# A Hymba block on one core: the first half's input projection on the input times the norm's weight, its row factors applied behind it, and another order of loads and background work

## The chip, the cores and the metric

One core of a Trainium2 chip runs the whole program. The time is device microseconds of one execution. The kernel before was run three times; its median is 2093.23 us.

## The reference

The kernel computes one decoder block in float32 on 2048 positions of width 1024. Cut to what matters for the change:

```python
h = rmsnorm(x, norm1_g)                    # x * rsqrt(mean(x^2) + 1e-6) * norm1_g
proj = h @ w_in
p_q, p_k, p_v, p_g, p_a, c_b, c_c, c_h = split(proj)

log_a = log_sigmoid(p_a @ w_gate_up + b_gate) / 16          # the gate
o = gla_chunked(q, k, v, log_a)            # chunks of 64, a state carried along
o = rmsnorm(o, gla_norm_g) * silu(p_g)
o_conv = c_b * causal_depthwise_conv(c_c * c_h, conv_w)     # width 3

x = x + concat([o, o_conv]) @ w_out
h2 = rmsnorm(x, norm2_g)
x = x + (silu(h2 @ w_ffn_gate) * (h2 @ w_ffn_up)) @ w_ffn_down
return rmsnorm(x, norm_f_g)
```

The norm's row factor rsqrt(mean(x^2) + 1e-6), one number for each position, can be taken out of the product: proj is that factor times ((x * norm1_g) @ w_in).

## The kernel before

**Arithmetic.** A float32 product is made of three matmuls in a rounded format: each operand is split into a high and a low half (`split`, lines 152 to 154: ACT copies the source into the high half, DVE subtracts that from the source for the low half), and TensorE adds high x high, high x low and low x high. A main matmul has 128x128 weights and 128x512 of the other operand.

**Units.** Positions are worked on in two halves of two blocks of 512. The input projection has twelve units (`unit`, the weights of one unit are 1 MB, four quarters of 128x512 each). Ten units of the first half and all of the second make a 2x2 block product from seven products of sums and differences (84 main matmuls); POOL makes the sums and differences of weights (`unit_weights`), and those of the operands are called T1 to T4. The first two units of the first half are plain, 96 main matmuls each: `build_first` (lines 288 to 328) makes the operands of the half as it goes and multiplies them, and `plain_unit` (line 330) is the second. The differences of the operands (line 325, POOL) are made behind these.

**The start.** `first_loads` (line 486) loads for each of the two blocks four tiles of rows (128x1024) and eight tiles of the transposed input (`h`, 128x512), with the first unit's weights between. ACT squares the rows and adds them up (line 484); `rows_rstd` (line 469) makes the row factor from these sums, spreads it over 128x128 tiles (`rep`, line 477) and transposes them on TensorE into a PSUM bank `rb_ps`. `scaled` (line 510, DVE) multiplies each h tile by the norm's weight and by that factor; the result is split into `op`, the operand of the first unit.

**Background work.** Python generators stand in a list; after each product a `tick` takes steps from the first of them. In the list stand the gate's weights, nine empty steps, `row_stats` of the second half's two blocks (row squares and factors), `gate(0)`, and `h1_ahead`, which makes the second half's operands, B11 to T4, and writes them to memory. `gate` has 32 matmuls into `a_ps` (line 578) and then eight into `z` (line 591); from z, `forget_gate` (lines 597 to 614) makes the decay by ACT and DVE with a scan (line 607) and stores it (`sd`). `gla_half` then runs through the first half's chunks: it loads kq, the decay `ee`, vt and gt (lines 695 to 707), DVE multiplies kq by the decay (lines 703 and 704), TensorE makes the scores `sc` (line 714) and transposes (lines 720 and 723), and so on.

**What sets the order.** The program is traced in Python's order and then scheduled once, at build time, by a simulated timeline; each engine runs its own instructions in that fixed order, and waits on semaphores. SP issues all loads and stores, in order, and blocks on the first that has to wait.

## Time and profile before

| | us |
|---|---|
| median of three executions | 2093.23 |
| the three executions | 2089.54, 2093.23, 2095.66 |
| the profiled execution | 2092.78 |
| its span | 2090.8 |
| start of TensorE's first main matmul | 18.43 |
| end of the second plain unit (192 main matmuls) | 78.5 |
| last main matmul of the first half's input projection (1032) | 288.5 |
| TensorE's granted clock over the span | 0.993 of full |

The span runs from the first to the last instruction of the profile; 2.0 us of the execution's time lie around it. A row of the profile names an engine (PE is TensorE, PEld its weight loads, DVE VectorE, ACT ScalarE, POOL GpSimd, SP SyncE), a line of the kernel, an operation and its tiles, output before input. A row of the timeline begins with its start and its length in us; "x2" behind it is the number of instructions that were put together, and in brackets stands how long the engine was idle before it and what ended that. A row of the waits names the waiting engine and line, the one it waited for, the sum in us, the number of waits and the longest. A row of the busy windows gives the window, its length, then each engine's busy time with its number of instructions, the granted clock, the share of the DMA engines and GB/s. TensorE's matmuls overlap, so the length of one in the timeline is longer than the step from one to the next.

### The profile page before, as it was taken

Reading aid. Unit: us, or ns where it says so; the run is one execution under the profiler, and the core shown is the slowest. Engines: PE = TensorE matmul, PEld = TensorE weight load, DVE = VectorE, ACT = ScalarE, POOL = GpSimd, SP = SyncE. Lnnn points to the kernel's source line nnn. Section 1 sums busy time; section 2 is a strip of 40 time slices with the busy share of each in tenths; the row PEclk is TensorE's granted clock in tenths of the full one; section 3 lists DMA queues with packets and bytes.
Section 4 is the critical chain, followed back from the end, with each engine's and each line's share of the span. In section 5 each row is a group of like instructions: output and inputs, shape, how many; then the busy total and the mean of one; then the engine's idle time right before and its main releaser. Section 6 shows DMA issues by size and latency. Waiting matters only on the chain.

```text
span 2090.8 us, 26872 instructions
## 1 busy us (share of the span) xinstructions
PE 2029.0 (97%) x9133; PEld 1648.4 (79%) x9133; DVE 1434.0 (69%) x2049; ACT 970.1 (46%) x1921; POOL 876.7 (42%) x637
## 2 busy tenths in 40 slices
PE   5999999999999999999999999999999999999996
PEld 4778888887888887778788878887888888878884
DVE  6669786549754696787887566654776767666665
ACT  5555455656543345454555442223455444453234
POOL 3427222122102464555555434533655544434543
PEclk9999999999999999999999999999999999999998
DMA  7349485424586882654654587698454465488672
GB/s 275 126 152 307 154 338 162 146 96 145 181 306 212 329 286 93 230 224 174 227 222 171 214 326 280 235 358 349 146 206 158 169 228 191 164 349 307 267 272 111
DMA packets 189241, 464.43 MB, mean 222 GB/s; under 512 B 19824, under 2 KB 65072, under 8 KB 179504
## 3 DMA queue, kind: packets, MB, share of 16 engines
q1 hardware_dynamic: 189104, 462.72, 61.3%
q8 instruction: 72, 1.18, 0.2%
q14 instruction: 65, 0.53, 0.1%
HBM read 297.49 MB, written 165.15 MB: 221 GB/s over the span
## 4 chain that ended last, share of the span: by engine, by line
PE 77%; DVE 10%; DMA 6%; issue 3%; ACT 2%; POOL 2%; SPq 1%; DVEq 0%; ACTq 0%; POOLq 0%
PE mm L381 22%; PE mm L383 22%; PE mm L382 22%; DVE wq L154 2%; DVE h L510 2%; PE mm L814 2%; PE mm L815 2%; PE mm L817 2%; DMA op<-shT 1%; DVE so L154 1%; DVE op L154 1%; PE a_ps L578 1%; DMA shT<-so 1%; SPq L145 1%; PE o_ps L738 1%
## 5 line engine op out<-in xcount | busy, mean ns | idle before, releaser
L381 PE MATMUL mm<-op,wq 128*128 128x512 f32 x2499 | 979.6, 394 | 11.0 <-ACT wq L153 4.2
L382 PE MATMUL mm<-op,wq 128*128 128x512 f32 x2499 | 974.5, 390 | 0.0
L383 PE MATMUL mm<-op,wq 128*128 128x512 f32 x2499 | 962.4, 391 | 11.7 <-DVE wq L154 11.2
L154 DVE TENSOR_TENSOR wq<-raw,wq 128x512 fp32r<-128x512 f32 (+2 forms) x626 | 506.7, 815 | 243.2 <-ACT wq L153 241.4
L153 ACT ACTIVATE wq<-raw 128x512 fp32r<-128x512 f32 (+2 forms) x626 | 365.0, 588 | 600.5 <-PE mm L383 461.9
L381 PEld LDWEIGHTS mm<-op,wq 128*128 128x128 f32 x2499 | 469.9, 188 | 123.4 <-ACT wq L153 10.3
L383 PEld LDWEIGHTS mm<-op,wq 128*128 128x128 f32 x2499 | 469.8, 188 | 119.8 <-DVE wq L154 21.5
L382 PEld LDWEIGHTS mm<-op,wq 128*128 128x128 f32 x2499 | 470.1, 188 | 96.5 <-issue 1.0
L366 POOL TENSOR_TENSOR raw<-s,raw 128x512 f32<-128x512 f32 (+2 forms) x97 | 126.5, 1304 | 468.2 <-DVE wq L154 446.9
L364 POOL TENSOR_TENSOR s<-raw 128x512 f32<-128x512 f32 (+2 forms) x97 | 127.2, 1311 | 219.5 <-DMA raw<-in_wffn_dram 95.1
L407 DVE TENSOR_TENSOR y<-mm,y 128x512 f32<-128x512 f32 x185 | 127.4, 689 | 123.3 <-PE mm L383 122.6
L371 POOL TENSOR_TENSOR raw<-raw 128x512 f32<-128x512 f32 (+2 forms) x97 | 125.4, 1292 | 166.0 <-DVE wq L154 158.8
L407 DVE TENSOR_TENSOR c<-mm,c 128x512 f32<-128x512 f32 x198 | 135.6, 685 | 64.6 <-PE mm L383 63.3
L796 POOL TENSOR_TENSOR ssx<-ssx,q 128x512 f32<-128x512 f32 x52 | 76.2, 1479 | 160.7 <-ACT q L795 160.5
L365 POOL TENSOR_TENSOR raw<-raw 128x512 f32<-128x512 f32 (+2 forms) x97 | 136.5, 1407 | 4.9
L403 ACT ACTIVATE c<-mm 128x512 f32<-128x512 f32 x198 | 114.8, 586 | 16.2 <-PE mm L383 14.8
L154 DVE TENSOR_TENSOR so<-t,so 128x512 fp32r<-128x512 f32 x100 | 90.9, 914 | 27.3 <-ACT so L153 26.7
L153 ACT ACTIVATE wq<-s 128x512 fp32r<-128x512 f32 (+2 forms) x97 | 56.8, 585 | 96.2 <-PE mm L383 92.7
L814 PE MATMUL mm<-op,wq 128*128 128x512 f32 x256 | 100.9, 395 | 0.0
L815 PE MATMUL mm<-op,wq 128*128 128x512 f32 x256 | 99.8, 390 | 0.0
L154 DVE TENSOR_TENSOR wq<-s,wq 128x512 fp32r<-128x512 f32 (+2 forms) x97 | 79.7, 822 | 4.1 <-ACT wq L153 3.5
L153 ACT ACTIVATE so<-t 128x512 fp32r<-128x512 f32 x100 | 62.4, 626 | 42.1 <-DMA sa_B<-so 17.8
(178 smaller groups left out, 1849.8 us busy)
## 6 DMA issues: line engine op xcount, KB each, us to landing
raw<-in_wffn_dram SPq DMA_DIRECT2D x44, 1024.0 KB, 5.7
sa_T<-so SPq DMA_DIRECT2D x88, 512.0 KB, 4.9
op<-sa_T SPq DMA_DIRECT2D x88, 512.0 KB, 8.9
sa_B<-so SPq DMA_DIRECT2D x69, 512.0 KB, 3.5
op<-sa_B SPq DMA_DIRECT2D x69, 512.0 KB, 9.2
raw<-in_win_dram SPq DMA_DIRECT2D x23, 1024.0 KB, 5.6
raw<-in_wdown_dram SPq DMA_DIRECT2D x24, 768.0 KB, 5.9
sx<-y SPq DMA_DIRECT2D x48, 256.0 KB, 3.2
```

Source lines behind the costliest of these rows:

```text
L153: last_hi[:] = [act.activation(hi, src, AF.Copy)]
L154: return dve.tensor_tensor(lo, src, hi.bitcast(F32), ALU.subtract)
L364: pool.tensor_tensor(s1, a21, a22, ALU.add)
L365: pool.tensor_tensor(a21, a11, a21, ALU.subtract)
L366: pool.tensor_tensor(a11, s1, a11, ALU.subtract)
L371: pool.tensor_tensor(a12, a12, a11, ALU.subtract)
L381: pe.matmul(o[:], wh, xh, start=first and k == 0, stop=False, skip_group_check=True)
L382: pe.matmul(o[:], wh, xl, start=False, stop=False, skip_group_check=True)
L383: return pe.matmul(o[:], wl, xh, start=False, stop=k == n - 1, skip_group_check=True)
L407: dve.tensor_tensor(t[:], o[:], t[:], ALU.add)
L814: pe.matmul(o[e, j][:], wh, m[:, 0, :], start=k == 0, stop=False)
L815: pe.matmul(o[e, j][:], wh, m[:, 1, :], start=False, stop=False)
```

## The change

The first half's projection no longer waits for the row factors: ACT and DVE split x times the norm's weight straight away (lines 317 and 320 of the changed file), and POOL scales the h tiles in place for the later differences (line 323). The row factor `factors` is multiplied in behind the product, only where a result needs it: on units 4, 5, 6 and 9 (`factored`, line 560; for 6 and 9 its square), on the gate's `a_sb`, on the convolution's y, on v (its square as ACT's scale) and in the GLA's own norm. q and k stay without it up to there. The loads come in another order (weights and h first, the second unit's weights ahead of the last h tiles, row tiles last), the row squares move into the background (`first_stats`), and 18 matmuls of 128x128 on a tile of ones stand ahead of everything. In the list of the background `gate(0)` is now last, behind all of `h1_ahead`.

```diff
-    def build_first(quad, w):
+    def build_first(h, raw):
 ...
+        def turn(n, i):
+            with ExitStack() as stack:
+                if order:
+                    stack.enter_context(tc.issue_after(order[-1].ins))
+                w[n] = weight_quarter(raw[:, i, :])
+            order.append(last_hi[0])
 ...
             for k in range(KD):
-                with ExitStack() as stack:
-                    if len(los) > 1:
-                        stack.enter_context(tc.issue_after(los[-2].ins))
-                    h[k, j] = quad(k, j)
+                g = col(C_G1 + k)
+                if j == 0 and k in (0, 3, 4):
+                    turn(*{0: ("A11", 0), 3: ("A12", 1), 4: ("A22", 2)}[k])
                 x = opp.tile([P, 2, PB], F32R, name="op", tag="op")
-                los.append(split(h[k, j][:], x[:, 0, :], x[:, 1, :]))
-                if j == 0 and k >= PT:
-                    row_squares(1, k - PT)
+                with tc.issue_after(order[-1].ins):
+                    order.append(act.activation(x[:, 0, :], h[k, j][:], AF.Copy, scale=g))
+                if (k, j) == (0, 0):
+                    turn("A21", 3)
+                dve.scalar_tensor_tensor(
+                    x[:, 1, :], h[k, j][:], g, x[:, 0, :].bitcast(F32), ALU.mult, ALU.subtract
+                )
+                pool.tensor_scalar(h[k, j][:], h[k, j][:], g, 1.0, ALU.mult, ALU.mult)
 ...
-            if j == 0:
-                rbs[1] = rows_rstd(squares[1])
+            out += [(r, j, settled(o[r, j], True), False) for r in range(2)]
 ...
+    def first_stats():
+        yield from pause(1)
+        for b in range(2):
+            for t in range(PT):
+                row_squares(b, t)
+                if t % 2:
+                    yield
+        yield from pause(3)
+        for b in range(2):
+            f, f2 = [mtiny.tile([P, PT], F32, name=n, tag=f"{n}{b}", bufs=1) for n in ("f", "ff")]
+            factors[b] = tiny.tile([P, PB], F32, name="rb", tag="rb")
+            act.activation(factors[b][:], rows_rstd(squares[b], f)[:], AF.Copy)
+            dve.tensor_tensor(f2[:], f[:], f[:], ALU.mult)
+            positions[b] = f, f2
+            yield
 ...
         raw = rawp.tile([P, 4, PB], F32, name="raw", tag="raw")
+        for j in range(2):
+            for k in range(KD):
+                if j == 0 and k % 4 == 0:
+                    for i in ((0, 3), (1, 2))[k // 4]:
+                        raw_loads.append(load(raw[:, i, :], win[0][:, i, :]))
+                if (j, k) == (1, 2):
+                    second = raw_weights(win[1])
+                h = raws[k, j] = bt("h") if len(raws) > 4 else tt("h")
+                load(h[:], xt[j, :, k, :])
 ...
+    def factored(c, in_psum, f):
+
+        s = tt("n") if in_psum else c
+        (dve if in_psum else pool).tensor_tensor(s[:], c[:], f[:], ALU.mult)
+        return s
 ...
         a_sb = bt("a_sb")
-        act.activation(a_sb[:], a[:], AF.Copy)
+        if half:
+            act.activation(a_sb[:], a[:], AF.Copy)
+        else:
+            for j in range(2):
+                r = slice(32 * j, 32 * j + 32)
+                dve.tensor_tensor(a_sb[r, :], a[r, :], factors[j][r, :], ALU.mult)
 ...
+        def values(u):
+            f = factors2 if u in (6, 9) else factors
+            for r, j, c, p in next(units):
+                if half == 0 and u in (4, 5, 6, 9):
+                    c, p = factored(c, p, f[j]), False
+                yield r, j, c, p
 ...
+                    if half == 0:
+                        pool.tensor_tensor(y[:], y[:], factors[j][:], ALU.mult)
 ...
-        act.activation(v[:], v_ps[:], AF.Copy)
+        if b in positions:
+            act.activation(v[:], v_ps[:], AF.Copy, scale=positions[b][1][:, t : t + 1])
+        else:
+            act.activation(v[:], v_ps[:], AF.Copy)
 ...
-            act.activation(sq[:], o[:, h, :], AF.Square, accum_out=ssq[:, h : h + 1])
+            f = positions[b][0][:, t : t + 1] if b in positions else 1.0
+            act.activation(sq[:], o[:, h, :], AF.Square, scale=f, accum_out=ssq[:, h : h + 1])
 ...
+    warm = bank("warm")
+    for _ in range(18):
+        pe.matmul(warm[:, 0:P], ones[:], ones[:], start=True, stop=True)
 ...
     background.extend(
         [
-            gate_weights(), pause(9), row_stats(2), row_stats(3), gate(0, ops), unhurried(),
-            h1_ahead(),
+            gate_weights(), first_stats(), pause(3), row_stats(2), row_stats(3), begun(h1, 10),
+            unhurried(), h1, gate(0, ops),
         ]
     )
```

Where instructions stand, at two places.

**The second unit's weights on ACT, early in the program.** Line 153 makes high halves (`wq` of weights, `op` of operands), line 484 or 515 squares rows, line 432 or 446 copies a result. Before, the last splits of the first unit's operands and the first two weights of the second unit:

```order
L153 ACTIVATE op_697<-h_512 128x512
L153 ACTIVATE op_707<-h_514 128x512
L464 ACTIVATE xn_1037,ssq_1036<-xn_1037 128x512
L153 ACTIVATE op_717<-h_516 128x512
L464 ACTIVATE xn_1038,ssq_1036<-xn_1038 128x512
L432 ACTIVATE c11_807<-mm_567 128x512
L153 ACTIVATE op_727<-h_518 128x512
L153 ACTIVATE wq_818<-raw_816 128x512
L153 ACTIVATE wq_821<-raw_816 128x512
```

And now, from the fourth of the eight row squares to the same two weights:

```order
L515 ACTIVATE xr_534,ssq_527<-xr_534 128x1024
L153 ACTIVATE op_734<-h_491 128x512
L515 ACTIVATE xr_537,ssq_536<-xr_537 128x1024
L153 ACTIVATE op_738<-h_493 128x512
L446 ACTIVATE c11_643<-mm_549 128x512
L515 ACTIVATE xr_539,ssq_536<-xr_539 128x1024
L446 ACTIVATE c11_645<-mm_550 128x512
L515 ACTIVATE xr_541,ssq_536<-xr_541 128x1024
L158 ACTIVATE rl_1000<-f_997 128x4
L153 ACTIVATE op_742<-h_495 128x512
L515 ACTIVATE xr_543,ssq_536<-xr_543 128x1024
L153 ACTIVATE wq_785<-raw_513 128x512
```

The row squares, which stood ahead of the first unit, stand between its last split and the second unit's first weights; op_734 and op_738 are splits of differences that POOL makes behind its scalings.

**The first half's gate and the first GLA chunk.** On TensorE, before, inside the eleventh unit, between its product on op_642 and its next one on op_773:

```order
L383 MATMUL mm<-op,wq 128x512
L714 MATMUL sc<-kq 128x128 x4
L720 MATMUL kt_ps<-ident,kq 128x128 x2
L723 MATMUL v_ps<-ident,vt 128x128 x2
L381 MATMUL mm<-op,wq 128x512
```

Now, ahead of the last product of the twelfth unit (op_922 to op_934, twelve matmuls), the last two z matmuls:

```order
L623 MATMUL z_2719<-a_sb_2591,wgu_sb_101 128x512
L623 MATMUL z_2761<-a_sb_2591,wgu_sb_101 128x512
L395 MATMUL mm_2545<-op_922,wq_2542 128x512
L396 MATMUL mm_2545<-op_922,wq_2542 128x512
L397 MATMUL mm_2545<-op_922,wq_2542 128x512
```

and behind that product the scores, followed by the second half's first matmul (op_2820 is its first operand):

```order
L397 MATMUL mm<-op,wq 128x512
L757 MATMUL sc<-kq 128x128 x4
L763 MATMUL kt_ps<-ident,kq 128x128 x2
L766 MATMUL v_ps<-ident,vt 128x128 x4
L395 MATMUL mm<-op,wq 128x512
```

On DVE, before, the two steps on the kq that these scores read (kq_2726) stand among the last steps of the convolution in the tenth unit (L655) and weight splits:

```order
L655 SCALAR_TENSOR_TENSOR c12_1818<-u_2046,sml_99,c12_1818 128x512 x2
L154 TENSOR_TENSOR wq_2081<-raw_2066,wq_2081 128x512
L703 TENSOR_TENSOR kq_2726<-kq_2726,ee_2727 128x256
L704 SCALAR_TENSOR_TENSOR kq_2726<-kq_2726,ee_2727 128x256
L154 TENSOR_TENSOR wq_2084<-raw_2066,wq_2084 128x512
```

Now the two steps on their kq (kq_2780), with the end of what stands between them and the step that reads z_2719 (thirty rows earlier); g2 is the decay, `op` the second half's operands:

```order
L643 TENSOR_TENSOR g2_2764<-g1_2763 128x512
L154 TENSOR_TENSOR op_2868<-op_2868 128x512
L154 TENSOR_TENSOR op_2872<-op_2872 128x512
L645 TENSOR_TENSOR dn_2717<-em_2716,el_2718 128x4
L154 TENSOR_TENSOR op_2876<-op_2876 128x512
L645 TENSOR_TENSOR dn_2717<-em_2716,el_2718 128x4
L154 TENSOR_TENSOR op_2880<-op_2880 128x512
L154 TENSOR_TENSOR op_2884<-op_2884 128x512
L154 TENSOR_TENSOR op_2888<-op_2888 128x512
L154 TENSOR_TENSOR op_2892<-op_2892 128x512
L154 TENSOR_TENSOR op_2896<-op_2896 128x512
L746 TENSOR_TENSOR kq_2780<-kq_2780,ee_2781 128x256
```

On SP the load of the second part of ee_2781 now stands behind two stores of the decay:

```order
L148 DMA sd1_1_131<-g2_2764 128x512
L145 DMA gt_2783<-sg0_2_154 128x128
L145 DMA gt_2783<-sg0_3_155 128x128
L145 DMA kq_2956<-sk0_0_112 128x128
L145 DMA ee_2781<-sd0_1_129 128x128
```

The gate's 32 a_ps matmuls and eight z matmuls, which stood behind main matmuls 312 to 384, stand now behind 938 to 1020. From main matmul 1056 on, TensorE's order is the same in both programs.

More of the change, by code (lines that the diff above doesn't have):

```diff
@@ L225, in unhurried, with begun @@
         yield
+    def begun(work, n):
+        for _ in range(n):
+            next(work)
+            yield
     def pause(n):
@@ L479, in rows_rstd @@
         return rb_ps
-    rbs, raws, first_weights, last_load, rows, squares = {}, {}, {}, [], {}, {}
+    rbs, raws, positions, rows, squares, factors, factors2 = {}, {}, {}, {}, {}, {}, {}
     def row_squares(b, t):
@@ L495, in first_loads @@
                 load(xr[:], x[r0 : r0 + P, :])
[L496 to L507 removed]
+        return raw, second
     def scaled(g, rb, h):
@@ L614, in forget_gate, with in_proj @@
         store(s_d[b][i][:], t2[:])
-    def in_proj(half, ops, first=None, differences=None):
+    def in_proj(half, ops, first=None, second=None, differences=None):
+        def values(u):
[4 more added lines that the diff above has]
+                yield r, j, c, p
         def units():
             for u in range(12):
-                with ExitStack() as stack:
-                    if half == 0 and u == 1:
-                        stack.enter_context(tc.issue_after(last_load[0].ins))
-                    if half or u > 1:
-                        us = unit(win[u], ops)
-                    else:
-                        us = plain_unit(win[u], ops) if u else first
+                if half or u > 1:
+                    us = unit(win[u], ops)
+                else:
+                    us = plain_unit(second, ops) if u else first
                 if half == 0 and u == 1:
```

58 lines of the change are left out of this document (26 added, 32 removed).

## The prediction

> **What bounds the kernel now.** First the busy times and the share of each engine in the chain that ended last, then the waits of TensorE:
>
> ```profile
> PE 2029.0 (97%) x9133; PEld 1648.4 (79%) x9133; DVE 1434.0 (69%) x2049; ACT 970.1 (46%) x1921; POOL 876.7 (42%) x637
> PE 77%; DVE 10%; DMA 6%; issue 3%; ACT 2%; POOL 2%; SPq 1%; DVEq 0%; ACTq 0%; POOLq 0%
> PE rb_ps L478 <- DVE rep L477: 15.7, 2, 15.5
> PE mm L383 <- DVE wq L154: 11.2, 10, 2.7
> ```
>
> TensorE works for 97% of the span, and two items carry most of its waiting: 15.5 us ahead of the first transposes (the row norm at the start) and 11.2 us in ten waits for low halves of weights. The busy windows of the part that the change reorders, cut where TensorE has issued 0, 96+96 (two plain units), 276, 864, 1032 and 1056 of its main 128x512 matmuls, say where that waiting lies (columns: length, then PE, PEld, DVE, ACT, POOL busy, granted clock, DMA share, GB/s):
>
> ```profile
> 0.00:18.40 18.40, 1.34 (x4) 0.65 (x4) 6.32 (x20) 9.02 (x17) 1.11 (x7) 1.00 0.87 299
> 18.40:78.50 60.10, 52.46 (x196) 40.16 (x197) 54.55 (x74) 39.67 (x94) 31.99 (x21) 0.94 0.64 222
> 78.50:97.80 19.30, 19.30 (x87) 15.93 (x87) 9.23 (x17) 6.36 (x11) 5.17 (x4) 1.00 0.31 110
> 97.80:248.80 151.00, 148.68 (x635) 118.74 (x635) 117.49 (x162) 75.78 (x140) 67.54 (x44) 0.99 0.63 209
> 248.80:288.50 39.70, 39.70 (x184) 32.60 (x183) 25.91 (x38) 16.77 (x35) 9.11 (x6) 1.00 0.61 235
> 288.50:295.50 7.00, 7.00 (x41) 5.78 (x39) 4.57 (x6) 2.79 (x7) 4.00 (x3) 1.00 1.04 401
> ```
>
> From 78.5 us on TensorE is full but for 2.3 us. One unit of 84 matmuls takes 19.3 us with its three transposes, or 0.227 us a matmul. Before that, 192 matmuls (43.6 us at this pitch) need 78.5 us: 34.9 us are lost, 18.4 of them before the first. In the second row DVE is busy for 54.55 of 60.10 us: there DVE, not TensorE, sets the pace.
>
> After main matmul 1056 the order of TensorE is the same in both programs to the last row. So the forecast is the time at which matmul 1056 is reached: 295.5 us now.
>
> **Two prices that the sum needs.** DVE and POOL hold each other up. The same split of 128x512 and the same three-element work of DVE, with POOL idle (first two rows) and with POOL at its differences (the rest):
>
> ```profile
> 27.75 1.29 DVE L154 TENSOR_TENSOR op<-h,op 128x512 fp32r<-128x512 f32 x2
> 27.46 0.16 DVE L472 TENSOR_SCALAR msq<-ssq 128x4 f32<-128x4 f32 x1
> 51.19 6.99 DVE L154 TENSOR_TENSOR op<-h,op 128x512 fp32r<-128x512 f32 x6
> 59.38 1.23 DVE L472 TENSOR_SCALAR msq<-ssq 128x4 f32<-128x4 f32 x1
> 47.26 5.16 POOL L325 TENSOR_TENSOR h<-h 128x512 f32<-128x512 f32 x3
> 54.25 6.33 POOL L325 TENSOR_TENSOR h<-h 128x512 f32<-128x512 f32 x4 [1.84 <-DVE op L154]
> ```
>
> A split costs DVE 0.65 us alone and 1.17 beside POOL; a difference costs POOL 1.6 to 1.7; a 128x4 operation rises from 0.16 to 1.23. Where both queues are full, I count a pair (one difference, one split) as 1.75 us and a small operation as 1.25.
>
> The new scaling on POOL (one 128x512 input, in place) has no row. Its nearest are one-input selects:
>
> ```profile
> 1.07 0.29 POOL masks.py:199 TENSOR_SCALAR_AFFINE_SELECT ident<-ident 128x128 f32<-128x128 f32 x1
> 1.40 0.41 POOL L80 TENSOR_SCALAR_AFFINE_SELECT mask<-mask 128x256 f32<-128x256 f32 x1
> 35.35 1.28 POOL L325 TENSOR_TENSOR h<-h 128x512 f32<-128x512 f32 x1 [33.54 <-DVE h L510]
> ```
>
> By the step from 128 to 256 columns it is 0.65 us, by twice the second row 0.82, and the two-input difference bounds it at 1.28. I take 0.8, nearest to the selects, and that it shuts DVE out as the differences do. The Trainium skill (GPSIMD Engine Reference, section 4.1 Engine selection) has one-input operations on GpSimd at roughly line rate; an estimate by that page, with DVE's 0.65 for such a tile as the line rate, ends the first unit below at 28 us and the sum 3 us lower. A rule of the Trainium skill that speaks against the change (SBUF — State Buffer, section Who interferes with whom): a DVE instruction with two SBUF inputs and a GpSimd instruction that reads SBUF share a pair of ports that one of them holds for its whole length; the 0.65 that became 1.17 agrees.
>
> **The first unit.** Removed: four row squares, a row norm and its four transposes ahead of matmul 0, four squares and the second norm inside the unit, and 16 scalings on DVE. What is left ahead of it is one weight quarter and one input tile, 512 KB, whose transfer runs at this rate:
>
> ```profile
> 4.00:6.00 2.00, 0.00 (x0) 0.00 (x0) 0.00 (x0) 1.11 (x2) 0.00 (x0) 1.00 0.98 381
> L484 ACT ACTIVATE xr<-xr x8: 1039/1050/1056, 4.9 to 26.1; 128x1024 f32<-128x1024 f32 x8
> ```
>
> That is 1.4 us of transfer behind the first issues; the first row square, on half a megabyte too, started at 4.9 us, and a split on ACT and DVE takes about 1.2 more, so matmul 0 stands at about 6 us instead of 18.4. Then DVE has 16 low halves and four weight low halves at 0.6, and POOL its 16 scalings at 0.8 between them: 20 x 0.6 + 16 x 0.8 = 24.8, so unit one ends at about 31 us (28 at 0.65, 38 at 1.28; TensorE alone would need 6 + 21.8 = 28). It ends now at 51.6. The 18 warm-up matmuls read a constant and run while nothing else can; nothing is counted for them.
>
> **The second unit gives part of it back.** Its first weights, wq_785, stand on ACT behind the 16 splits and eight row squares, which have moved from the start to here, and behind splits of differences that POOL can begin only after the scalings. A square (1.05 above) with the read of its sum costs 1.2:
>
> ```profile
> 22.33 0.18 ACT L484 ACTIVATION_READ_ACCUMULATOR xr<-xr 128x1 f32 x1
> ```
>
> Sixteen splits end near 20 us, eight squares and the splits between them add 15: wq_785 at 35 to 36 us, though its megabyte lands near 14 (4.5 MB stand ahead of its end, 12 us at 381 GB/s, behind 2 us). The row's 48 matmuls run from 37.5 to 48.5. The other row's weights, wq_857, have their low half on DVE behind nine 128x4 or 64-column operations and three pairs with POOL: 9 x 1.25 + 3 x 1.75 = 16.5 after 37, so 53.5; 48 x 0.227 = 10.9 follow, and matmul 192 stands at 65 (60 if the small operations run at 0.6, 72 if unit one is long). Against 78.5 that gains 13.5 us.
>
> The next unit's third weights, wq_953, stand on ACT behind the 16 row squares of the second half and on DVE behind four differences; I put them at 75 us, ten after the unit begins, and the unit at 24.3 instead of 19.3 (19.3 if covered, 28).
>
> **The middle.** The gate's 32 a_ps matmuls and its eight z matmuls leave it, and stand between 864 and 1032 now:
>
> ```profile
> 455.83 7.63 PE L578 MATMUL a_ps<-op,wa_sb 128*128 128x512 f32 x32
> 468.83 1.12 PE L591 MATMUL z<-a_sb,wgu_sb 32*128 32x512 f32 x2
> 472.82 1.12 PE L591 MATMUL z<-a_sb,wgu_sb 32*128 32x512 f32 x2
> 476.11 3.49 SPq L148 DMA_DIRECT2D sd<-g  x2
> 477.16 1.37 DVE L607 TENSOR_TENSOR_SCAN g<-ones,g 128x128 f32<-128x128 f32 x4
> 483.53 1.12 PE L591 MATMUL z<-a_sb,wgu_sb 32*128 32x512 f32 x2
> 494.19 0.41 DVE L703 TENSOR_TENSOR kq<-kq,ee 128x256 f32<-128x256 f32 x1
> 495.68 0.71 PE L714 MATMUL sc<-kq 64*128 64x128 f32 x8
> ```
>
> They cost 7.6 + 4 x 1.03 = 11.7 us wherever they stand, so 151.0 becomes 139.3 and 39.7 less its 1.6 of scores and transposes plus 11.7 becomes 49.8. The new products with the row factors (POOL on SBUF tiles, DVE on PSUM ones, two ACT squares) fall into these 190 us; in the first 151 DVE is busy for 78% and POOL for 45%, so its idle time covers them, at nothing. The 139.3 holds 4 us of waiting beside its 588 matmuls (133.5) and 16 transposes; without any it is 136, with twice as much 143.
>
> **The gate's new place.** This is the term against the change. TensorE's last two z matmuls stand ahead of the last product of the twelfth unit, 12 matmuls or 2.7 us; behind it come the scores of the first chunk, and only behind these the second half's matmuls, whose operands are loaded by then. TensorE takes its rows in order, so whatever the scores wait for, all of the second half waits for too. They wait for kq_2780, the thirtieth row on DVE behind the g2 that reads z. Those rows are six steps of the gate and its two scans of four, the convolution's last two products and three splits, one weight split, twelve splits of the second half's operands, three 128x4 products and the two of kq: 24 x 0.6 + 2 x 1.37 + 3 x 0.15 + 2 x 0.41 = 18.4 us, without any meeting with POOL. On SP the load of its decay, ee_2781, also stands behind two stores that wait for those scans. None of these rows can start before z. From z to its scan the rows above take 477.16 - 472.82 = 4.3 us, of which DVE's own two steps are 1.2 and what is ACT's about 2.8, so sc waits 18.4 + 2.8, less 2.7 of the product: 18.5 us. From both sides: 14.5, if the splits ahead of the scans run before z is there; 25, from the second half's own gate, where sc stands 26.8 us behind the first z of the three rows above and 22.8 behind the second. In the program before, the last z stands 600 main matmuls (136 us) ahead of sc: the wait is not there.
>
> A pause of TensorE has a price of its own. After the transposes it sat idle for 1.7 us, and the stretch behind ran at half clock:
>
> ```profile
> 33.70:36.00 2.30, 0.59 (x4) 0.36 (x3) 1.84 (x5) 0.74 (x2) 0.65 (x1) 1.00 0.98 368
> 36.00:39.40 3.40, 3.25 (x7) 2.15 (x8) 3.40 (x4) 1.59 (x5) 3.40 (x3) 0.50 0.68 241
> ```
>
> Half of 3.4 is 1.7 us. So matmuls 1032 to 1056 take 18.5 + 1.5 (scores, transposes) + 1.7 + 24 x 0.227 = 27.1 instead of 7.0 (23.1 to 33.6).
>
> **The sum.** 65 + 24.3 + 139.3 + 49.8 + 27.1 = 305.5 against 295.5: 10.0 us later, 2092.8 + 10 = 2103 us, with the 2.0 us around the span as they are. The profiled execution lies 0.4 under the median of the runs shown, so no correction. All terms at their low ends give 288.2 (2086), all at their high ends 326.4 (2124).
>
> **Rivals.** (1) *The front gains more than the gate takes.* If the pair price holds only for differences and the scalings hide in DVE's gaps, unit one ends at 28, wq_857 comes at 45 and matmul 192 at 56; with the gate's wait at 14.5 the sum is 56 + 24.3 + 139.3 + 49.8 + 23.1 = 292.5: 2090, a result that cannot be told from no change. For it: DVE's 54.55 of 60.10 falls by 16 scalings of 0.66. Against: wq_857's queue is a count of rows, whatever the scalings cost. (2) *TensorE does not wait at the scores.* If DVE and SP have finished most of the list when z arrives, that is if the splits and products stand done and only the chain z, ACT, scan, store, load of 8 us remains, the wait is 5 us (8 less 2.7), no half clock follows, and with the unit behind matmul 192 covered too the sum is 65 + 19.3 + 139.3 + 49.8 + 12 = 285.4: 2083, faster. For it: the splits need no z. Against: DVE takes its rows in order too, and 12 of them stand between the scans and kq. (3) *Contention is dearer.* POOL has the 32 scalings and differences, then unit weights and row factors without a gap; if pairs cost 1.75 also with a scaling, unit one ends at 38, matmul 192 at 72, the next unit takes 28 and the gate waits 25: 72 + 28 + 139.3 + 49.8 + 33.6 = 322.7, 2120. It decides from a scaling of about 1.1 us on. (4) *The change doesn't do what it says*: weights load sooner but are split no sooner. That is already in the 35 us of wq_785; if squares and row tiles delay it to 45, matmul 192 stands at 75 and the result is 2113.
>
> **How the numbers follow.** Chances: the forecast 0.45, rival 1 0.2, rival 2 0.17, rivals 3 and 4 together 0.18. About 0.3%, 6 us, can be told from no change. The forecast with its own range, 2096 to 2112, is slower in nearly all of its cases (the rest same); rival 1 is mostly same, with a part on either side; rival 2 faster; rivals 3 and 4 slower. That gives faster 0.20, same 0.20, slower 0.60. The range that leaves out 2 in 10 reaches from rival 2's 2083 to just under rival 3's 2120: 2084 to 2117.
>
> **What would show it.** In the changed profile: matmul 0 near 6 us and matmul 96 near 31 (the first term); TensorE's longest wait in the first 80 us on wq of the second unit, with ACT's L515 squares ahead of it (the second); POOL's L323 with a mean of 0.8 (the third); one wait of TensorE on DVE's kq, 14 to 25 us, at about 280 us, and half clock behind it (the gate); the rest of the trace shifted by a constant. The forecast is wrong if TensorE passes the scores with a wait under 10 us, if matmul 192 stands before 58 us, or if something behind matmul 1056 moves by more than 3 us, which no term here holds.

## The result, and the profile after

| | us |
|---|---|
| before, median of 4 | 2091.39 (2087.8 to 2095.66) |
| changed, median of 4 | 2117.28 (2115.41 to 2121.68) |
| ratio | 1.013, 95% interval 1.0112 to 1.0148 |
| profiled execution of the changed kernel, its span | 2117.62, 2115.9 |

The change makes the kernel 26 us slower; the forecast was 10 us slower, and the range ended 0.3 us short. Its profile, by the same views. The page's busy row, then TensorE's waits up to 330 us (waiting engine and line, what it waited for, us in total, times, longest):

```profile
PE 2036.7 (96%) x9169; PEld 1657.2 (78%) x9169; DVE 1438.1 (68%) x2049; ACT 976.7 (46%) x1920; POOL 926.7 (44%) x673
```

```profile
PE sc L757 <- DVE kq L747: 23.7, 1, 23.7
PE mm L395 <- ACT c L417: 14.4, 4, 8.8
PE mm L395 <- ACT wq L153: 5.4, 1, 5.4
```

These waits, 46 us with the small ones, stand where the kernel before waited 26.7 us up to 295.5: 15.7 for transposes, 4.2 for low halves of weights (the prediction's 11.2 us in ten waits are those of the whole run) and 6.8 for the rest. The busy windows, cut at the first main matmul and at matmuls 96, 192, 276, 864, at the last one ahead of the scores, and at 1056 (same columns as in the prediction):

```profile
0.00:7.51 7.51, 6.11 (x37) 5.92 (x37) 2.82 (x9) 2.69 (x4) 1.11 (x7) 1.00 0.64 208
7.51:36.01 28.50, 22.98 (x97) 17.78 (x97) 23.71 (x23) 23.20 (x42) 26.41 (x23) 0.99 0.98 371
36.01:61.12 25.11, 25.10 (x96) 20.02 (x97) 23.72 (x30) 14.34 (x37) 20.04 (x13) 0.87 0.50 163
61.12:92.29 31.17, 22.40 (x93) 17.89 (x92) 15.59 (x34) 18.59 (x45) 7.72 (x6) 0.84 0.52 178
92.29:237.20 144.91, 137.95 (x597) 111.43 (x596) 108.92 (x131) 62.01 (x112) 91.68 (x59) 0.99 0.55 193
237.20:287.40 50.20, 50.20 (x209) 38.37 (x207) 36.18 (x52) 22.92 (x46) 19.51 (x14) 1.00 0.57 209
287.40:321.73 34.33, 10.61 (x56) 8.65 (x55) 23.66 (x45) 15.26 (x34) 2.98 (x2) 0.65 0.69 239
```

Beside the terms of the sum:

| main matmuls | before | forecast | measured |
|---|---|---|---|
| to 192 | 78.5 | 65 | 61.1 |
| 192 to 276 (third unit) | 19.3 | 24.3 (19.3 to 28) | 31.2 |
| 276 to 864 (the middle) | 151.0 | 139.3 (136 to 143) | 144.9 |
| 864 to 1032, without the wait | 39.7 | 49.8 | 50.2 |
| 1032 to 1056, with the wait | 7.0 | 27.1 (23.1 to 33.6) | 34.3 |
| sum | 295.5 | 305.5 | 321.7 |

Behind matmul 1056 the two spans are 1795.3 and 1794.2 us long: all of the difference is here. The front gains 17.4 us; 11.9 go in the third unit, and the gate's new place takes 27.3 where the forecast had 20.1. Against the forecast the terms are off by -3.9, +6.9, +5.6, +0.4 and +7.2 us, 16.2 in all.

### The profile page after: what moved, and what is told of

Its sections match the earlier page's. It is cut to its first block, busy times and chain, and to the rows that moved or that the text cites. A ratio compares the mean times of both kernels' runs of the same rounds, so it can differ in the third digit from the quotient of the medians.

```text
span 2115.9 us, 27026 instructions
## 1 busy us (share of the span) xinstructions
PE 2036.7 (96%) x9169; PEld 1657.2 (78%) x9169; DVE 1438.1 (68%) x2049; ACT 976.7 (46%) x1920; POOL 926.7 (44%) x673
## 4 chain that ended last, share of the span: by engine, by line
PE 79%; DVE 9%; DMA 6%; issue 3%; ACT 2%; POOL 1%; SPq 1%; DVEq 0%; ACTq 0%; POOLq 0%
PE mm L395 23%; PE mm L397 23%; PE mm L396 23%; DVE wq L154 2%; PE mm L863 2%; PE mm L864 2%; PE mm L866 2%; DVE h L539 1%; DVE so L154 1%; DMA h<-in_xt_dram 1%; DVE op L154 1%; DMA op<-shT 1%; PE a_ps L605 1%; PE o_ps L784 1%; PE o_ps L786 1%
## 5 line engine op out<-in xcount | busy, mean ns | idle before, releaser
L154 DVE TENSOR_TENSOR wq<-raw,wq 128x512 fp32r<-128x512 f32 (+2 forms) x626 | 514.2, 826 | 238.1 <-ACT wq L153 235.9
L417 ACT ACTIVATE c<-mm 128x512 f32<-128x512 f32 x198 | 114.9, 586 | 13.3 <-PE mm L397 11.9
L154 DVE TENSOR_TENSOR so<-t,so 128x512 fp32r<-128x512 f32 x100 | 88.8, 893 | 27.3 <-ACT so L153 26.9
L153 ACT ACTIVATE so<-t 128x512 fp32r<-128x512 f32 x100 | 62.5, 626 | 38.4 <-DMA sa_B<-so 16.6
```

The lines of the kernel that those rows point to most:

```text
L153: last_hi[:] = [act.activation(hi, src, AF.Copy)]
L154: return dve.tensor_tensor(lo, src, hi.bitcast(F32), ALU.subtract)
```

## The experiments

Stage times are read from each run's own profile at the same main matmuls. A time without an interval is that of one execution, in which 3 or 4 us say little. A ratio is taken against the kernel before as it ran beside that experiment (medians of 2090 to 2092 us).

**Is it the gate's place?** Two edits of the background list: the changed kernel with the gate early (e1), and the kernel before with the gate last (e2).

```diff
 e1: ... row_stats(2), row_stats(3),
+    gate(0, ops),
     begun(h1, 10), unhurried(), h1,
-    gate(0, ops),
 e2: gate_weights(), pause(9), row_stats(2), row_stats(3),
-    gate(0, ops),
     unhurried(), h1_ahead(),
+    gate(0, ops),
```

> The changed kernel with gate(0) back in its old place in the background list (ahead of the second half's operands); all else as changed. Theory A: the gate's new place is the loss. TensorE's 23.7 us wait for kq and the half clock behind it (about 3 us) go, and the total is 2117 - 27 = 2090, level with the kernel before. Theory B: the front's gain was never real at the end, and the gate's steps only meet DVE's full list earlier: the wait goes but 10 us or more come back between main matmuls 276 and 528, total 2100 or more.

> The kernel before with nothing changed but gate(0) put last in the background list. Theory A: the same wait at the scores appears, a little longer because no product stands between z and the scores: 27 us and 3 us of half clock, total 2092 + 29 = 2121. Theory B (the wait belongs to the changed kernel's other edits): total under 2100.

e2: 2115.24 us, ratio 1.0117 (1.01 to 1.0134), with the wait at the scores:

```profile
PE sc L714 <- DVE kq L704: 25.8, 1, 25.8
```

The gate's place alone makes a kernel without any other edit 24 us slower: theory A, 5 us smaller than expected (in its own order the first two units end 4 us sooner, at 74.4). e1: 2113.06 us, ratio 1.0106 (1.0087 to 1.0124), from three executions; a fourth took 7247.06 us, for a reason that its record does not show, and is in neither number. The wait at the scores is gone, and matmuls 276 to 864 take 176.6 us: theory B. So the gate at its old place in the list is no cure, and e1's own profile says why for the larger part. Table loads on ACT between 110 and 180 us in e1, by line (silu L456, the gate's exponentials and logarithms the rest):

```profile
L456 ACT ACT_TABLE_LOAD x5 | 6.4, 1283 | 0.1
L635 ACT ACT_TABLE_LOAD x4 | 5.1, 1283 | 0.1
L634 ACT ACT_TABLE_LOAD x3 | 3.8, 1283 | 0.1
L642 ACT ACT_TABLE_LOAD x2 | 2.6, 1283 | 0.0
L644 ACT ACT_TABLE_LOAD x1 | 1.3, 1283 | 0.0
```

Fifteen loads of 1.28 us: with the front earlier, the silu products (units 5 and 6) come while the gate, which waits in the list for the row squares, is still at its z, and ACT changes its table at every turn. ACT is busy for 29.04 of the 32.10 us around it, and TensorE waits there:

```profile
159.02 0.80 PE L395 MATMUL mm<-op,wq 128*128 128x512 f32 x1 [9.43 <-ACT wq L153]
```

In the kernel before, the gate's last logarithm leaves ACT 8 us ahead of the first silu, and three loads do for the same stretch. Beside the changed kernel, these matmuls (276 to 864) take 31.7 us more: 11.7 are the gate's own matmuls, 11.7 are lost in this stretch (matmuls 444 to 528), and 7.1 between 612 and 864, where DVE is the full engine (28.45 of 28.60 us in the longest unit).

**Squares later, with the gate early.**

```diff
-gate_weights(), first_stats(), pause(3), row_stats(2), row_stats(3), gate(0, ops),
+gate_weights(), first_stats(), pause(9), row_stats(2), row_stats(3), gate(0, ops),
```

> e1 with nine empty steps instead of three ahead of the second half's row squares. Theory A: the 8.8 us wait of the third unit for ACT's copy c11 comes from the sixteen row squares ahead of it on ACT; without them there main matmul 276 stands at about 81 instead of 92 us, total 10 us under e1. Theory B: the squares are only put ahead of another copy and delay it as much: total within 3 us of e1.

2121.72 us, ratio 1.0145 (1.013 to 1.016): neither. Matmul 276 stands at 91.8 (216 at 74.6: the squares still stand ahead of the copy), and everything from 444 to 864 is late. Six empty steps do not move the squares, and the gate meets the silu products as in e1 (14 table loads between 60 and 260 us).

**The gate ahead of the squares.**

```diff
-gate_weights(), first_stats(), pause(3), row_stats(2), row_stats(3), begun(h1, 10),
-unhurried(), h1, gate(0, ops),
+gate_weights(), first_stats(), gate(0, ops), row_stats(2), row_stats(3),
+begun(h1, 10), unhurried(), h1,
```

> The changed kernel with gate(0) directly behind first_stats in the background list, ahead of the second half's row squares, so that its z matmuls stand behind main matmuls 264 to 276, well ahead of the silu products, and the squares come later. Theory A: the gate then costs its 11.7 us of TensorE time only, meets no silu (no table loads between, against 15 of 1.28 us in the kernel with the gate at its old place in the list), and the third unit's wait behind the squares goes; the front keeps some 12 of its 17 us, the row factors cost 6: total about 2085. Theory B: DVE and POOL have no room left in the middle, and whatever is moved there from the end or the front is paid in waits for weights between main matmuls 360 and 864: total 2100 or more.

2090.84 us over 10 executions, ratio 0.9996 (0.9983 to 1.0009): all 26 us are back with one entry of the list moved and three empty steps left out, and nothing beyond. The gate costs its own 11.7 us, ACT loads two tables between 60 and 260 us, and matmul 216 stands at 66.4 instead of 75.7: the third unit's wait is gone with the squares. But the front's 17.7 us at matmul 192, still 18 at 528, are 3.8 at 864: theory B's place for the rest, though not its 2100 us. The stretch that takes them, matmuls 612 to 864, and its worst unit:

```profile
175.42:245.08 69.66, 60.15 (x253) 46.37 (x252) 62.36 (x69) 27.23 (x55) 45.18 (x28) 1.00 0.58 194
198.84:223.99 25.15, 19.93 (x86) 15.53 (x84) 25.11 (x30) 9.43 (x22) 17.05 (x9) 1.00 0.60 186
```

DVE is busy for 25.11 of 25.15 us there, and its rows are stretched beside POOL's: a split of 0.68 us takes 1.75 to 1.77.

**What the row factors cost.** Left out of the changed kernel (e8), left out of e7 (e10), moved to DVE in e7 (e12). e8 and e10 leave the factor out of the silu products, the convolution and the output.

```diff
 e8, e10:
-                if half == 0 and u in (4, 5, 6, 9):
-                    c, p = factored(c, p, f[j]), False
...
-                    if half == 0:
-                        pool.tensor_tensor(y[:], y[:], factors[j][:], ALU.mult)
 e12:
-        (dve if in_psum else pool).tensor_tensor(s[:], c[:], f[:], ALU.mult)
+        dve.tensor_tensor(s[:], c[:], f[:], ALU.mult)
...
-                        pool.tensor_tensor(y[:], y[:], factors[j][:], ALU.mult)
+                        dve.tensor_tensor(y[:], y[:], factors[j][:], ALU.mult)
```

> The changed kernel without the products with the row factor on units 4, 5, 6 and 9 and on the convolution's y (the silu products, the convolution and so the output are left without it). Theory A: these 24 products, most on POOL with DVE shut out, are the 6 us that the middle is too long: main matmuls 276 to 864 take 137 to 139 us instead of 144.9 and the total falls by 6. Theory B: they are covered, and the 4.4 us wait near 182 us is the second half's operands on the same engines: 143 to 145 us, total unchanged.

> e7 (gate ahead of the squares) without the products with the row factor on units 4, 5, 6 and 9 and on the convolution's y, which leaves the silu products, the convolution and the output without it. Theory A: with the gate out of the way, what takes back the front's gain between main matmuls 612 and 864 (69.7 us in e7, 57.2 at TensorE's pitch) are these products, 20 of them on POOL for 33 us with DVE shut out: the stretch takes 57 to 61 us and the total is about 2079. Theory B: it is the second half's operands, squeezed into fewer units: 66 us or more, total 2086 or more.

> e7 with all products with the row factor on DVE (about 0.65 us each) instead of POOL (1.5 to 1.9 each, with DVE shut out). Theory A: what counts is the time for which DVE and POOL shut each other out, which falls by 20 x 0.9 = 18 us: the stretch from main matmul 612 to 864 gets 5 to 10 us shorter, total about 2083. Theory B: DVE is the full engine there (25.16 of 25.20 us in the worst unit) and gets 13 us more work: total 2093 or more.

e8: the middle takes 139.24 us (its row below), total 2112.19: theory A, 5.7 us. e10: matmuls 612 to 864 take 58.0 us instead of 69.7, as A says, at the pitch of TensorE (second row). Against e7, 5.3 us are given back in the unit ahead of 612, where TensorE waits 4.2 us for ACT's copy, and the single run is 2084.26: 5 us above A's 2079, so of the 16.3 us that e7's front loses on the way to matmul 1056, the row factors explain 6.3, and the rest stays open. e12: 65.4 us (third row), total 2089.22, ratio 0.9999 (0.9989 to 1.0008): 4.3 of the 11.7 us are had by moving the products off POOL, less than A's 5 to 10, 3.3 are lost again ahead of 612, and the time of the whole can't be told from e7's.

```profile
92.53:231.77 139.24, 136.58 (x598) 112.02 (x596) 96.04 (x128) 62.64 (x113) 63.44 (x44) 0.99 0.57 200
```

```profile
180.73:238.73 58.00, 57.76 (x253) 47.15 (x252) 48.21 (x63) 26.44 (x53) 28.48 (x19) 1.00 0.62 206
```

```profile
178.67:244.04 65.37, 60.78 (x253) 47.91 (x252) 59.58 (x74) 26.15 (x52) 28.91 (x19) 0.97 0.55 182
```

**What holds the scores.** The forecast's 18.5 us were DVE's thirty rows. Four experiments on the changed kernel: the decay's load from ACT's queue (e6), the twelve splits of the second half's operands put behind kq on DVE (e9), and with e9 the decay's load from POOL for one chunk (e11) and for two (e15). The edit of e9 also takes one more step of the background list ahead of the second half, so in these three the second half's gate stands 34 matmuls earlier.

```diff
 e6:
-                load(dst[:, i, :], r[:, s])
+                if src is s_d[b] and (b, t) == (0, 0):
+                    nc.scalar.dma_start(dst[:, i, :], r[:, s])
+                else:
+                    load(dst[:, i, :], r[:, s])
 e9:
-        split(o[:, 1, :].bitcast(F32), o[:, 0, :], o[:, 1, :])
+        hi, lo = o[:, 0, :], o[:, 1, :]
+        act.activation(hi, lo.bitcast(F32), AF.Copy)
...
+                stack.enter_context(tc.issue_after(first_kq[0].ins))
+            dve.tensor_tensor(lo, lo.bitcast(F32), hi.bitcast(F32), ALU.subtract)
 e11, on e9, as in e6 but:
+                    nc.gpsimd.dma_start(dst[:, i, :], r[:, s])
 e15, on e11:
-                if src is s_d[b] and (b, t) == (0, 0):
+                if src is s_d[b] and b == 0 and t < 2:
```

> The changed kernel with the first chunk's two loads of the decay (ee) issued from ACT's queue instead of SP's. Theory A: the last part of the wait at the scores is SP's queue: DVE had ended its list 3.1 us before the decay came. Then kq follows DVE's list at once and the wait falls from 23.7 to about 20.5 us. Theory B: the load waits for the stores of the decay themselves or for the busy DMA engines, wherever it is issued: wait 23 to 24 us.

> The changed kernel with the low halves of the second half's twelve operands T3, B22 and T4 put behind the first chunk's kq on DVE (7.2 us of rows). Theory A: DVE's list is what the scores wait for: the wait falls by the 7.2 us to about 16.5. Theory B: SP's queue, with the decay's load behind the stores of the last scan and some ten other issues, holds kq just as long: wait 21 to 23.5 us.

e6: 23.5 us. The load was issued at 305.65 us, 2 us earlier, but ACT's own work waited behind it: the last three high halves came late, DVE's last splits ended at 308.59 instead of 307.33, and kq followed them at once. It tells nothing of SP. e9: 24.1 us. DVE, without the splits, sits idle for 10.27 us ahead of kq:

```profile
310.49 0.42 DVE L752 TENSOR_TENSOR kq<-kq,ee 128x256 f32<-128x256 f32 x1 [10.27 <-ACT ee L750]
```

Theory B, 0.6 us beyond its bound, and against the forecast's own reason. What SP does in those 10 us, in e9:

```profile
303.11 0.89 SPq L148 DMA_DIRECT2D sd<-g  x2
304.06 1.71 SPq L145 DMA_DIRECT2D vt<-sv  x3
305.81 1.85 SPq L145 DMA_DIRECT2D gt<-sg  x4
307.71 0.43 SPq L145 DMA_DIRECT2D kq<-sk  x1
308.18 0.43 SPq L145 DMA_DIRECT2D ee<-sd  x1
```

The stores of the last scans are issued from 303.1 on, and the load waits for another eight issues, of about 0.5 us each.

> e9 (splits behind kq) with the first chunk's loads of the decay issued by POOL, which has nothing to do there, instead of SP. Theory A: SP's queue alone held the decay (DVE sat idle for 10.3 us ahead of kq in e9): the wait at the scores falls from 24.1 to 14 to 17 us. Theory B: the stores of the decay, or DMA engines that are busy, hold it wherever it is issued: 21 us or more.

> e11 with the decay's loads of the first two chunks on POOL's queue, so that ACT's exponentials of neither chunk wait for SP. Theory A: SP's order is what holds the scores: the wait falls from 25 to 17 to 18 us (the decay lands near 302 us). Theory B: another engine's order holds them just as long: 21 us or more.

e11: 25.4 us, but not by B: kq's first product ran at 302.3, and its second waited until 310.2 for an exponential that stands on ACT behind the next chunk's, whose decay still came through SP. e15: 18.7 us, with both products of kq done by 305.2 (A said 17 to 18, B 21 or more):

```profile
305.29 1.22 PE L768 MATMUL sc<-kq 64*128 64x128 f32 x8 [18.67 <-DVE kq L756]
```

With the splits out of the way, SP's order held the scores for 5.4 us more than the rest of the chain needs. SP's order relieved with DVE's list as it is, which e6 was to show, was not measured. The totals of the four (2120.32, 2125.08, 2126.74 and 2119.36) are no lower, since in e9, e11 and e15 the next step waits: 5.3 to 7.5 us of TensorE on the masked scores, which stand on DVE behind the splits.

**Is the wait lost time?** The changed kernel with the scores nine products later (e16), and with two more edits (e17).

```diff
 e16:
-        background.append(gla_half(half))
+        background.extend([gla_half(half)] if half else [pause(4), gla_half(half)])
...
-    drain_background(lambda: len(background) < 2)
+    drain_background(lambda: len(background) < 3)
...
+                    if (b, t) == (0, 0):
+                        stack.enter_context(tc.issue_after(last_product[0].ins))
 e17, on e16, with the factors as in e12 and:
-                act.activation(xn[:], xn[:], AF.Square, accum_out=ssq[:, t, e : e + 1])
+                with tc.issue_after(last_hi[0].ins):
+                    act.activation(xn[:], xn[:], AF.Square, accum_out=ssq[:, t, e : e + 1])
```

> The changed kernel with the gate last as it is, but the first chunk's scores put behind nine products of the second half (main matmul 1140 instead of 1032). Theory A: the 23.7 us and the half clock behind them are lost only because TensorE's order has the scores ahead of matmuls whose operands are loaded: main matmul 1056 stands at 293 to 296 us, total 2117 - 26 = 2091. Theory B: the wait moves to the second half's own splits and weights on DVE, or the chunks come late for the output projection: total 2100 or more.

> e16 with two more edits: the row-factor products on DVE instead of POOL, and the second half's row squares put behind the weights that are split when they are traced. Theory A: the third unit's 9 us wait goes (main matmul 276 at 81 to 84 us instead of 92), the middle loses 2 to 4 us less, and with the scores out of the way the front's gain arrives: total 2077 to 2083, faster than both. Theory B: the squares make the second half's operands late, and DVE, full between 612 and 864, takes it back: total 2088 or more.

Both halves of A's mechanism are there, and neither total. Matmul 1056 stands at 292.8 us in e16 and at 288.8 in e17 (276 at 81.5, as A says), 2.7 and 6.7 ahead of the kernel before; but between matmuls 1700 and 3000 both lose 23 to 24 us against it, and end at 2111.53, ratio 1.0096 (1.0082 to 1.011), and 2108.86, ratio 1.0081 (1.0067 to 1.0095). The first chunk's scores come behind 1140 matmuls instead of 1032, the chunks, the second half's gate and its chunks follow one another in the one background list, and in e16 the last transposes of that chain stand behind 2387 matmuls instead of 2291. Where each of these us is lost was not followed further; over these matmuls TensorE is idle for 12.8 us in e16 and for 3.2 before, nearly all of e16's in one wait of 6.1 us behind the second gate, at 520 us, and two of 2.6 and 3.8 at 800.

**The first two units.** The scalings left out (e4: the differences are made of unscaled tiles), the squares put behind the second unit's weights in e12 (e14), the warm-up left out (e5).

```diff
 e4:
-                pool.tensor_scalar(h[k, j][:], h[k, j][:], g, 1.0, ALU.mult, ALU.mult)
 e14: e12 and
-        yield from pause(1)
+        yield from pause(4)
...
-                row_squares(b, t)
+                with tc.issue_after(last_hi[0].ins):
+                    row_squares(b, t)
 e5:
-    for _ in range(18):
-        pe.matmul(warm[:, 0:P], ones[:], ones[:], start=True, stop=True)
```

> The changed kernel without POOL's sixteen scalings of h (the differences T1 to T4 of the first half are then made of unscaled tiles, so the units behind the second compute something else). Theory A: the scalings, at 1.13 us each with DVE shut out, set the pace of the first unit; without them main matmul 96 stands at 29 instead of 36 us and matmul 192 at 54 to 56 instead of 61, but the third unit's wait for ACT takes most of it back: matmul 276 at 88 to 92, total 2113 to 2118. Theory B: DVE's own list or the loads set the pace: matmul 96 at 34 to 36.

> e12 with the first half's row squares put behind the second unit's weights on ACT. Theory A: the 6.3 us wait for wq_785 comes from these squares: main matmul 96 stands at 31 to 33 instead of 36 us and 192 at 55 to 57 instead of 61, and the total is 4 to 5 us under e12. Theory B: the squares are then late for the gate and the silu products, and what was gained is waited for there: total at or above e12.

> The changed kernel without its 18 warm-up matmuls. Theory A: DVE sets the pace of the first unit, and the warm-up is worth nothing: matmul 96 at 36 us as before the edit, total within 3 us. Theory B: the first matmuls then run at half the granted clock and the first unit ends 2 to 3 us later.

e4: matmul 96 at 38.4, 192 at 66.6, total 2112.98: neither theory. The first unit's last matmul starts at 29.97 us instead of 30.26, so neither the scalings nor DVE's list set this unit's pace (more below). With the scalings out, POOL turns to the differences at once, and beside these a low half takes 1.65 us on DVE instead of 1.17; the second unit is the later for it. e14: 96 at 32.0 and 192 at 57.5 as A says, and 2098.69 us, ratio 1.004 (1.0027 to 1.0054): theory B, the squares delay the row factors, and with them the gate (now behind 276) and the second half's operands (the first is scaled at 141.2 us instead of 121.4). e5: 2113.25 us, matmul 48 at 21.2 instead of 19.6, 96 at 35.0 instead of 36.0: nothing lost at matmul 96, as A says, but not for A's reason. B's half pace is there (from matmul 2 to 9 TensorE's steps are 0.43 us instead of 0.23, though the clock column reads 1.00) and the unit's last matmul starts 1.6 us later; the wait for the second unit's weights, 2.7 us instead of 5.4, takes it up.

## Why the prediction was wrong

The sign, the place and the main mechanism held: slower, through one wait of TensorE on kq behind the gate's new place, with the front's gain too small to pay for it. The size fell short by 16 us, in three terms of the sum.

- **"So sc waits 18.4 + 2.8, less 2.7 of the product: 18.5 us"** was 23.7, and with the half clock behind it the stretch was 34.3 instead of 27.1, above its bound of 33.6. The step that failed is to take DVE's list for the limit: the load of the decay was seen "also" behind two stores and given no time. These rows show it in the changed kernel: SP issues it at 307.80, DVE is idle for 3.1 us, and kq is done 4 us behind DVE's list. These 3.1 us are the larger part of the 5.2 that were missing; the other 2 are in the list itself, which was counted "without any meeting with POOL".

```profile
304.90 0.38 SPq L148 DMA_DIRECT2D sd<-g  x1
305.32 0.43 SPq L145 DMA_DIRECT2D gt<-sg  x1
305.85 0.38 SPq L148 DMA_DIRECT2D sd<-g  x1
306.27 0.94 SPq L145 DMA_DIRECT2D gt<-sg  x2
307.26 0.49 SPq L145 DMA_DIRECT2D kq<-sk  x1
307.80 0.43 SPq L145 DMA_DIRECT2D ee<-sd  x1
```

```profile
310.43 0.42 DVE L746 TENSOR_TENSOR kq<-kq,ee 128x256 f32<-128x256 f32 x1 [3.10 <-ACT ee L744]
```

  DVE's rows ahead of kq begin with L633 and end with the five splits:

```profile
286.64 1.78 DVE L154 TENSOR_TENSOR wq<-raw,wq 128x512 fp32r<-128x512 f32 x1
288.94 0.74 DVE L633 TENSOR_SCALAR g<-z,sml 128x512 f32<-128x512 f32 x1
294.54 2.38 DVE L639 TENSOR_TENSOR_SCAN g<-ones,g 128x128 f32<-128x128 f32 x4
304.24 3.09 DVE L154 TENSOR_TENSOR op<-op 128x512 fp32r<-128x512 f32 x5
```

  They took 18.4 us, from 288.94 to 307.33, where the forecast had 17.6 (its 18.4 hold the two products of kq, 0.8): beside POOL one scan took 2.38 us instead of 1.37. They began 1.3 us into the wait where the forecast had 0.1, behind rows that POOL had stretched, such as the 1.78 us of the first line. e9 shows that without DVE's splits the wait stays, e15 that with SP's queue out of it too it falls.
- **"the unit at 24.3 instead of 19.3"** was 31.2. The squares were named, and the time at which they let go was right (ACT's copy c at 75.1, forecast 75 for wq_953), but the work that they hold up was the copy of the unit's first result, not only its third weights, so TensorE stood still for 8.8 us, and paid at half clock behind it. Since the unit began 4 us sooner than forecast, its end is only 3 us off. e7 and e17, with the squares elsewhere, show the wait gone.

```profile
66.60:75.70 9.10, 0.36 (x3) 0.12 (x1) 5.30 (x13) 8.59 (x23) 0.56 (x1) 0.68 0.67 257
75.70:79.20 3.50, 3.48 (x8) 2.80 (x9) 2.36 (x6) 1.12 (x2) 0.70 (x1) 0.50 0.00 0
```

- **"its idle time covers them, at nothing"** was 5.7 us (e8), a term that was mis-sized by taking a mean over 151 us for room at the place. The products stand in the units in which DVE and POOL are also at the second half's operands; in e7 they cost 11.7 us between matmuls 612 and 864 (e10), of which 6.4 are left at 864.

What held: matmul 0 at 7.5 us (about 6), the second unit's first matmul at 36.0 (37.5), the gate's matmuls (50.2 for 49.8), and nothing behind matmul 1056. In the list of signs, "matmul 96 near 31" is the end of the first unit; counted as everywhere here, matmul 96 is that of 36.0. TensorE's longest wait in the first 80 us was not on the second unit's weights (5.4 us) but in the third unit.

Two numbers of the front came out right for another reason than the forecast's, which is luck:

- The first unit's end, 30.6 us (31). It was added up from DVE's and POOL's rows, 24.8 us. But the 95 steps between the unit's matmuls took 22.75 us, and at 0.227 us each they would take 21.6: TensorE was at its own pitch but for 1.2 us, and began 1.5 us later than forecast.
- Matmul 192, 61.1 us (65, from 60 to 72). The wait for wq_857 up to 53.5 us is not there: TensorE is busy for 25.10 of the second unit's 25.11 us. What is there in its place is half clock behind the wait of 5.4 us, which the forecast counted at the scores and not here:

```profile
36.01:42.00 5.99, 5.98 (x13) 4.29 (x14) 5.99 (x6) 4.44 (x14) 5.99 (x4) 0.50 0.10 31
42.00:61.12 19.12, 19.12 (x84) 15.73 (x84) 17.73 (x25) 9.90 (x25) 14.05 (x10) 0.99 0.62 205
```

POOL's scaling took 1.12 us where DVE was in its way, and 0.69 where DVE was idle, against the forecast's 0.8 for both. It overlaps with the low half on DVE: twelve of these stand 1.17 us apart, where the forecast had 1.4 for a pair. The 0.69 agrees with the Trainium skill (GPSIMD Engine Reference, section 4.1 Engine selection), by which one-input operations run there at roughly line rate: a split of such a tile on DVE takes 0.69 too.

```profile
L323 POOL TENSOR_SCALAR h<-h,sml x16: 689/1118/1644, 8.3 to 30.9; 128x512 f32<-128x512 f32 x16
```

Rival 3 came closest in its total, 2120, in part by another way: its third unit (28 us) and its stretch at the scores (33.6) are near the measured 31.2 and 34.3, but its front (38 us for the first unit, 72 at matmul 192) did not come, although the scaling took the 1.1 us that was to decide for it. Rivals 1 and 2 counted on waits of 14.5 and 5 us at the scores, against 23.7.

## What to carry to other kernels

A wait that a reordering creates ends with the last of several in-order queues: write each of them out to the waiting instruction, the DMA-issuing one at its own price per issue (0.45 us here) and ACT's with the next chunk's rows, and take the latest. A factor that is taken out of a product has to be put in somewhere: price it in the unit where it lands, by what DVE and POOL do there, not by their mean over the stage. Background work with its own function table on ACT can be cheap at one place in the list and dear at another (two table loads in e7, fifteen in e1): when the front moves, look where the gate meets the silu before anything else. A stage time that comes out right is no proof of its sum: look at which engine was full.

## What the runs showed of the hardware

A table load on ACT takes 1.28 us, and nine of e1's fifteen lie in the stretch of 32.1 us in which TensorE was busy for 22.0. The Trainium skill (ScalarE: Activation LUTs, section What ACT_TABLE_LOAD costs) has the same 1283 ns, and a drain of about 1380 ns beside it, which no row of e1 shows: the next operation starts 1.3 us after the start of the load. A wait of TensorE of 9.1 us was followed by 3.5 us at a granted clock of 0.50; the 23.8 us at the scores (0.59 over them) by 0.50 and 0.65 for the next 5.4:

```profile
287.40:311.20 23.80, 0.28 (x2) 0.00 (x0) 20.68 (x39) 10.93 (x24) 2.98 (x2) 0.59 0.91 319
311.20:313.20 2.00, 1.80 (x11) 1.60 (x12) 0.61 (x3) 0.83 (x2) 0.00 (x0) 0.50 0.47 137
313.20:316.60 3.40, 3.40 (x14) 2.85 (x13) 1.03 (x3) 1.07 (x2) 0.00 (x0) 0.65 0.36 95
316.60:321.00 4.40, 4.40 (x25) 3.77 (x23) 0.69 (x1) 1.70 (x4) 0.00 (x0) 1.00 0.00 0
```
